# A gated attention and spatial-gating block on one core: reciprocal roots of the norms on GpSimd instead of VectorE and ScalarE

## The chip, the cores and the metric

The kernel runs on one core of one Trainium2 chip. The metric is the device time of one execution in microseconds; lower is better. The engines are named as the profile names them: PE (TensorE, matmuls; PEld is its weight load), DVE (VectorE), ACT (ScalarE), POOL (GpSimd) and SP (SyncE, which here only issues DMAs). Each engine takes its instructions in the order in which they stand in its own queue, and waits on semaphores for the others.

## The reference

One layer of a hybrid block on a sequence of 1024 rows of 1024 features, all in float32. Three norms take a reciprocal root, and they are what the change is about.

```python
def rmsnorm(x, g):
    y = xf * lax.rsqrt(jnp.mean(xf * xf, axis=-1, keepdims=True) + EPS)
    return (y * g)

def layernorm(x, g, b):
    xc = xf - mean(xf)
    return xc * lax.rsqrt(jnp.mean(xc * xc, axis=-1, keepdims=True) + EPS) * g + b

def reference(...):
    h = rmsnorm(x, norm_g)                             # norm 1
    q, k, v, za, u, vs, zs, gm = split(h @ w_in)
    a = window_sink_attention(rope(q), rope(k), v, sinks)
    a = (a * silu(za)) @ w_att_out
    sgo = gelu(u) * (mix(layernorm(gelu(vs))) + b)     # norm 2
    sgo = (sgo * silu(zs)) @ w_sg_out
    ga, gs = sigmoid(gm + b_merge)
    x = x + (ga * a + gs * sgo) @ w_o
    return rmsnorm(x, final_g)                         # norm 3
```

## The kernel before

Rows are handled in eight tiles of 128 (`NT` = 8, P = 128 partitions). A float32 matrix product is made of three matmuls of reduced-precision parts: each operand is split into a high part (a cast, on ACT, L155 or L554) and a low part (the difference, on DVE, L156 or L555), and PE multiplies high by high, high by low and low by high. The larger products go through `gemm_pair` (L350), which makes a two-by-two block product with seven instead of eight block products; its operands are sums, made beforehand. A scheduling layer places the instructions: the source fixes what depends on what, and the layer decides in which order the instructions of each engine stand, from its own estimates of what each costs. `after` (L158) adds an order between two instructions where the source asks for one.

The stages that touch the three norms:

- *Start.* Four dummy matmuls (`keep_busy`, L498) and the spreading of the gain row over partitions (L505). For each row tile t, `scale_of` (L528) squares the tile on ACT and sums the squares (L531, with a read of the accumulator), and `rstd_of` (L130) makes the reciprocal root; `normed_tile` (L537) scales the two halves of the tile on DVE (L545), PE transposes them (L551, two PSUM banks in turn), ACT and DVE make the high and low part (L554, L555), and ACT keeps an unsplit copy (L558, or L615 for tile 0). `vs_gemm` (L588) multiplies the first half of the `vs` columns with each tile: 24 matmuls (L596), whose result ACT copies out (L597). The weights for it are split in `split_vs` (L573): the first quarter in two halves, one on DVE and one on POOL (L583), the other three by L155 and L156.
- *Middle.* The second half of the `vs` columns is one long run of matmuls (L565). GELU follows on ACT (L637, L701), then the statistics per row on DVE (L633, L737), `normalize` (L739) with one reciprocal root for all eight tiles at once (128x8), and eight scalings (L742). The mixing matmuls (L764) read the result. Meanwhile POOL issues DMAs that add up weight blocks (L296), paced so that each waits for a given step of PE or ACT.
- *End.* The output product runs in four passes p of two row tiles each, seven block products a pass. After each block product `add_and_square` (L1582) adds the residual on DVE (L1584), squares the half on ACT and sums it (L1586); the first half's sum is scaled and offset (L1593), the second half's goes into `rstd_of` with the first as its base. `scale_and_store` (L1596) multiplies by root and gain (L1606 on DVE) and stores; in the last pass one half of each tile has its gain multiplied beforehand on POOL (L1589) and takes the root on ACT (L1603). The stores of the first three passes are issued by POOL, those of the last one by SP and ACT.

`rstd_of` is a chain over two engines: scale and offset on DVE (L133), square root on ACT (L135), reciprocal on DVE (L137), and a refining step on DVE (L140 to L145) that makes up for the table's error. Where ACT's loaded table does not hold the function that comes next, a table load stands ahead of it; the first, for the root, is brought forward by a dummy (L108).

Of the kernel before, what the change touches and what calls it, by code (L numbers as in the profile page):

```python
# [24 lines left out]
F32 = mybir.dt.float32  # L25
F32R = mybir.dt.float32r
AF = mybir.ActivationFunctionType
ALU = mybir.AluOpType
PSUM = bass.MemoryType.PSUM

P = 128
D = 1024
# [3 lines left out]
NT = S // P  # L36
HD = 64
EPS = 1e-6
# [14 lines left out]
def hybrid_tile(  # L53
# [16 lines left out]
    nc = tc.nc  # L70

    dram = ctx.enter_context(tc.tile_pool(name="dram", bufs=1, space=bass.MemoryType.DRAM))
    const = ctx.enter_context(tc.tile_pool(name="const", bufs=1))
# [5 lines left out]
    def nm(s):  # L79
        count[0] += 1  # L80
        return f"{s}_{count[0]}"

    def bank(tag, dt=F32):
        return psum.tile([P, 512], dt, name=nm("ps_" + tag), tag="ps_" + tag, bufs=2)

    def mtile(shape, dt, tag, bufs, pool=None):
        return (pool or main).tile(shape, dt, name=nm(tag), tag=tag, bufs=bufs)
# [16 lines left out]
    make_identity(nc, ident[:])  # L104
    eps_sb = const.tile([P, 1], F32, name="eps_sb")
    nc.gpsimd.memset(eps_sb[:], EPS)
    warm = const.tile([P, 1], F32, name="warm")
    nc.scalar.activation(warm[:], eps_sb[:], AF.Sqrt)  # L108

    sink_sb = const.tile([P, 8], F32, name="sink_sb")  # L110
    nsink_sb = const.tile([P, 8], F32, name="nsink_sb")
# [15 lines left out]
    a_dr = scratch("a_dr")  # L127
    y_dr = scratch("y_dr")

    def rstd_of(ss, scale, base=EPS, n=1):  # L130

        ve = mtile([P, n], F32, f"st{n}", 16 if n == 1 else 5)
        nc.vector.tensor_scalar(ve[:], ss, scale, base, op0=ALU.mult, op1=ALU.add)  # L133
        rt = mtile([P, n], F32, f"st{n}", 16 if n == 1 else 5)
        nc.scalar.activation(rt[:], ve[:], AF.Sqrt)  # L135
        r0 = mtile([P, n], F32, f"st{n}", 16 if n == 1 else 5)
        nc.vector.reciprocal(r0[:], rt[:])  # L137
        e = mtile([P, n], F32, f"st{n}", 16 if n == 1 else 5)
        if n == 1:
            nc.vector.scalar_tensor_tensor(e[:], ve[:], r0[:], r0[:], op0=ALU.mult, op1=ALU.mult)  # L140
        else:
            nc.vector.tensor_mul(e[:], ve[:], r0[:])
            nc.vector.tensor_mul(e[:], e[:], r0[:])
        nc.vector.tensor_scalar(e[:], e[:], -0.5, 1.5, op0=ALU.mult, op1=ALU.add)
        nc.vector.tensor_mul(e[:], e[:], r0[:])  # L145
        return e

    def split(hi, lo, src, minus=False):
        if minus:
# [8 lines left out]
    def after(second, first):  # L158

        tc.add_manual_dep(  # L160
            second.ins,
            first.ins.name,
            mybir.DependencyInfo(mybir.DependencyClass.NoSync, mybir.DependencyReason.DATA),
            reason="order",
        )
# [5 lines left out]
    def slot(name, shape=(P, 4, HALF), dt=F32R):  # L171

        return mtile(list(shape), dt, "T_" + name, 1)
# [309 lines left out]
    mv = mtile([P, NT, 2], F32, "mv", 1, gelu)  # L483

    def load_x(t):
        xt = raw_tile()
        nc.sync.dma_start(xt[:], x[t * P : (t + 1) * P, :])
        return xt

    x_in = {0: load_x(0)}  # L490
    junk = mtile([P, D], F32, "wl", 3)
# [23 lines left out]
    f = {n: slot(at, dt=F32) for n, at in (("f11", "t3l"), ("f21", "t4l"))}  # L515
# [12 lines left out]
    def scale_of(t):  # L528
        xt = x_in[t] if t in x_in else load_x(t)
        ss = mtile([P, 1], F32, "st1", 16)  # L530
        square = nc.scalar.activation(junk[:], xt[:], AF.Square, accum_out=ss[:])  # L531
        if t == 1:

            after(square, casts[-1])
        return xt, rstd_of(ss[:], 1.0 / D)

    def normed_tile(t, scale=None):  # L537
        xt, r = scale or scale_of(t)
# [67 lines left out]
    x_in[1] = load_x(1)  # L606
    split_vs(1)
    second = scale_of(1)
    for c in (2, 3):
        load_vs(c)  # L610
# [126 lines left out]
        nc.vector.bn_aggr(mv[:, t, :], stats[:, t])  # L737

    def normalize():  # L739
        r = rstd_of(mv[:, :, 1], 1.0, n=NT)  # L740
        for t in range(NT):
            nc.vector.tensor_scalar(  # L742
                xh[:, t, :], xh[:, t, :], mv[:, t, 0:1], r[:, t : t + 1], op0=ALU.subtract, op1=ALU.mult
            )
# [574 lines left out]
    def gtag(among=4):  # L1319
        turn[0] += 1  # L1320
        return f"g{turn[0] % among}"
# [249 lines left out]
    for p in range(4):  # L1571
        n, t, acc, x11 = N_PAIRS + p, T_ORDER[p], accs[p], firsts[p]
# [3 lines left out]
        sq = {}  # L1576
# [5 lines left out]
        def add_and_square(i, half, src, sign):  # L1582
            z = xr[:, 2 * i + half, :]
            pace[0] = (nc.vector.tensor_sub if sign < 0 else nc.vector.tensor_add)(z, z, src)  # L1584
            ss = mtile([P, 1], F32, "st1", 16)
            nc.scalar.activation(bank("tp")[:], z, AF.Square, accum_out=ss[:])  # L1586
            if p == 3 and i == half:
                scaled[i, half] = mtile([P, HALF], F32, gtag(), 1, pool)
                nc.gpsimd.tensor_tensor(scaled[i, half][:], z, g_out[:, half, :], op=ALU.mult)  # L1589
            if i in sq:  # L1590
                sq[i] = rstd_of(ss[:], 1.0 / D, sq[i][:])
            else:
                nc.vector.tensor_scalar(ss[:], ss[:], 1.0 / D, EPS, op0=ALU.mult, op1=ALU.add)  # L1593
                sq[i] = ss

        def scale_and_store(i, p=p, t=t, xr=xr, sq=sq, scaled=scaled):  # L1596
# [34 lines left out]
        def by_t3():  # L1631
            product(acc, ready[n, 4], ob["t3"], False)
            make_sums(nc.vector.tensor_add(x22[:], x22[:], acc))
            add_and_square(1, 1, x22[:], -1.0)
# [111 lines left out]
```

## Time and profile before

| | us |
|---|---|
| three runs | 923.66, 924.23, 921.37 |
| their median | 923.66 |
| span of the profiled execution | 921.3 |
| PE busy in it | 904.7 |
| DVE busy | 691.5 |
| ACT busy | 521.8 |
| POOL busy | 126.8 |

The page states no time of the profiled execution beside its span; of the three runs the shortest, 921.37, is about as long as that span. Times in the views count from the start of the span. A row of the timeline gives start, duration, engine, line, operation, output and input, and in brackets how long the engine had been idle and what released it; rows of small operations that stand together can be merged (x2, x8). A row of the grouped view gives the busy time in total, the mean of one in nanoseconds, and the idle time ahead of the group with its releaser. The chain of waits is followed back from the last instruction.

### The profile page before, as it was taken

To read this page: it belongs to the slowest core of one execution; us is meant where nothing else is said; L and a number is where in the kernel's file an instruction comes from. 1 tells how busy PE (TensorE), PEld (TensorE's weight loads), DVE (VectorE), ACT (ScalarE), POOL (GpSimd) and SP (SyncE) were. 2 spreads that over 40 slices of the span, in tenths; PEclk is the share of its full clock that TensorE was granted. 3 is DMA by queue.
4 is the path that set the end of the run, shared out by engine and by line. 5 is a ranking of instruction groups with operands and counts; after the bars stand their busy time and mean duration, and the time that the engine had idled before them with its cause. 6 is when DMAs were issued, how large, how long until landed. Compare 5 with 4: busy or idle time off the path is not lost.

```text
span 921.3 us, 13177 instructions
## 1 busy us (share of the span) xinstructions
PE 904.7 (98%) x4332; PEld 752.7 (82%) x4332; DVE 691.5 (75%) x1241; ACT 521.8 (57%) x1046; POOL 126.8 (14%) x188
## 2 busy tenths in 40 slices
PE   8999999999999999999999999999998999999996
PEld 5888888888888788888888888888877887878885
DVE  6875776656687668887778888747798589579996
ACT  6862443334444366767766766755665385367443
POOL 0002122213011001211101111101100111110012
PEclk9999999999999999999999999999999999999998
DMA  6427678877788676776786799689869755998632
GB/s 240 138 91 215 207 197 184 161 158 234 230 290 267 229 200 182 169 202 184 197 240 222 248 220 253 174 313 349 294 219 341 240 201 151 272 307 303 206 115 114
DMA packets 128734, 201.71 MB, mean 219 GB/s; under 512 B 12345, under 2 KB 60729, under 8 KB 128666
## 3 DMA queue, kind: packets, MB, share of 16 engines
q1 hardware_dynamic: 109512, 148.17, 48.8%
q0 software_dynamic: 19008, 52.44, 23.8%
q8 instruction: 34, 0.56, 0.3%
q14 instruction: 34, 0.28, 0.1%
q10 hardware_dynamic: 146, 0.27, 0.1%
HBM read 144.07 MB, written 86.11 MB: 250 GB/s over the span
## 4 chain that ended last, share of the span: by engine, by line
PE 85%; DVE 8%; DMA 4%; issue 2%; ACT 1%; SPq 1%; DVEq 0%; ACTq 0%
PE ps_mm L341 34%; PE ps_o L341 25%; PE ps_mm L596 5%; PE ps_sc L1076 3%; PE ps_o L1161 2%; PE ps_tp L341 2%; PE ps_tp L1120 2%; PE ps_sc L341 2%; PE ps_tp L764 2%; DVE wl L156 1%; PE ps_tp L565 1%; PE ps_sc L565 1%; PE ps_o L565 1%; PE ps_mm L565 1%; DVE bq L185 1%
## 5 line engine op out<-in xcount | busy, mean ns | idle before, releaser
L155 ACT CAST wh<-s 128x1024 fp32r<-128x1024 f32 (+1 forms) x78 | 78.1, 1005 | 87.2 <-PE ps_mm L341 49.9
L156 DVE TENSOR_TENSOR wl<-wr,wh 128x1024 fp32r<-128x1024 f32 (+1 forms) x80 | 75.7, 948 | 49.1 <-ACT wh L155 48.3
L155 ACT CAST wh<-wr 128x1024 fp32r<-128x1024 f32 (+1 forms) x80 | 66.3, 830 | 71.6 <-PE ps_mm L341 34.3
L156 DVE TENSOR_TENSOR wl<-s,wh 128x1024 fp32r<-128x1024 f32 (+1 forms) x78 | 90.9, 1166 | 9.3 <-ACT wh L155 9.2
L341 PE MATMUL ps_o<-T_t1h,wh 128*128 128x512 f32 x148 | 58.9, 398 | 0.8 <-ACT wh L155 0.7
L341 PE MATMUL ps_o<-T_b22h,wh 128*128 128x512 f32 x148 | 58.2, 394 | 0.0
L341 PE MATMUL ps_o<-T_t1h,wl 128*128 128x512 f32 x148 | 57.9, 391 | 0.3 <-DVE wl L156 0.3
L341 PE MATMUL ps_o<-T_b22l,wh 128*128 128x512 f32 x148 | 57.9, 391 | 0.0
L341 PE MATMUL ps_o<-T_b22h,wl 128*128 128x512 f32 x148 | 57.8, 390 | 0.0
L341 PE MATMUL ps_o<-T_t1l,wh 128*128 128x512 f32 x148 | 57.6, 390 | 0.0
L341 PE MATMUL ps_mm<-T_b11h,wl 128*128 128x512 f32 x140 | 54.8, 392 | 2.9 <-DVE wl L156 2.9
L341 PE MATMUL ps_mm<-T_t4h,wh 128*128 128x512 f32 x140 | 55.3, 395 | 0.5 <-DVE x L376 0.5
L341 PE MATMUL ps_mm<-T_t3l,wh 128*128 128x512 f32 x140 | 54.6, 390 | 0.6 <-DVE T_t3l L156 0.6
L341 PE MATMUL ps_mm<-T_t2h,wl 128*128 128x512 f32 x140 | 55.0, 393 | 0.0
L341 PE MATMUL ps_mm<-T_t2l,wh 128*128 128x512 f32 x140 | 55.0, 393 | 0.0
L341 PE MATMUL ps_mm<-T_b11h,wh 128*128 128x512 f32 x140 | 54.9, 392 | 0.0
L341 PE MATMUL ps_mm<-T_t3h,wh 128*128 128x512 f32 x140 | 54.9, 392 | 0.0
L341 PE MATMUL ps_mm<-T_t2h,wh 128*128 128x512 f32 x140 | 54.7, 391 | 0.0
L341 PE MATMUL ps_mm<-T_t4h,wl 128*128 128x512 f32 x140 | 54.7, 391 | 0.0
L341 PE MATMUL ps_mm<-T_t3h,wl 128*128 128x512 f32 x140 | 54.7, 390 | 0.0
L341 PE MATMUL ps_mm<-T_b11l,wh 128*128 128x512 f32 x140 | 54.6, 390 | 0.0
L1089 ACT ACTIVATE pr<-ps_sc,sm 128x192 f32<-128x192 f32 (+2 forms) x128 | 50.9, 410 | 6.5 <-DVE sm L1085 5.5
(356 smaller groups left out, 2399.6 us busy)
## 6 DMA issues: line engine op xcount, KB each, us to landing
wr<-in_w_dram SPq DMA_DIRECT2D x86, 256.0 KB
sums<-in_w_dram POOLq DMA_DIRECT2D x20, 512.0 KB, 5.6
s<-sums SPq DMA_DIRECT2D x20, 512.0 KB
q_hl<-qhl SPq DMA_DIRECT2D x16, 512.0 KB
q<-q_hl SPq DMA_DIRECT2D x64, 128.0 KB
wr<-in_w_dram SPq DMA_DIRECT2D x14, 512.0 KB
y_dr<-x POOLq DMA_DIRECT2D x28, 256.0 KB, 6.6
g<-in_w_dram POOLq DMA_DIRECT2D x12, 512.0 KB, 7.2
```

Of the source, the lines that this page charges most:

```text
L155: nc.scalar.copy(hi, src)
L156: return nc.vector.tensor_sub(lo, src, hi.bitcast(F32))
L185: op(dst[:, i : i + 2, :], a[:, i : i + 2, :], c[:, i : i + 2, :])
L341: nc.tensor.matmul(acc, lt, rt, start=fresh and k == 0 and n == 0, stop=k == 3 and n == 2, skip_group_check=True,)
L565: mm = nc.tensor.matmul(acc, lt, rt, start=k == 0 and n == 0, stop=k == KC - 1 and n == 2)
L596: nc.tensor.matmul(acc[:], lt, rt, start=k == 0 and n == 0, stop=k == KC - 1 and n == 2)
L764: nc.tensor.matmul(pm[:, t * P : (t + 1) * P], xh[:, half * 4 + t, g * P : (g + 1) * P], bias[-1][1][:, g % 4, :], start=True, stop=True,)
L1076: nc.tensor.matmul(sc[:, i, k0:], q_of[:, c, i * P : (i + 1) * P], kt[:, f, k0:], start=f == 0, stop=f == 1,)
L1089: nc.scalar.activation(held_in[c, i], sc[:, i, lo:hi], AF.Exp, bias=nmax[:, c, i : i + 1], scale=-1.0, accum_out=sums[:, c, i : i + 1],)
L1120: nc.tensor.transpose(dst, pr[:, i, block * P : block * P + width], ident[:])
L1161: nc.tensor.matmul(po[:, cs], lt, rt, start=n == 0, stop=n == len(terms) - 1)
```

## The change

The reciprocal root is made on POOL by an addition of the offset and a power with exponent -0.5, the exponent read from a small tile filled once. The division by the number of features goes into the scale that ACT applies before it squares. The refining step, the square root on ACT and the reciprocal are gone. The dummy that loads a table at the start now asks for GELU's. The first half's sum in the last norm takes its offset on POOL too. In the built program the scheduling layer has placed the instructions of the start anew on every engine; from the first `gemm_pair` on the order is the same but for the operations named here, one sum (L245) that now stands behind the scalings L742, and the squares L1586 that stand ahead of the copies L1614 at the end of a pass.

```diff
     nc.gpsimd.memset(eps_sb[:], EPS)
+    power = const.tile([P, NT], F32, name="power")
+    nc.gpsimd.memset(power[:], -0.5)
     warm = const.tile([P, 1], F32, name="warm")
-    nc.scalar.activation(warm[:], eps_sb[:], AF.Sqrt)
+    nc.scalar.activation(warm[:], eps_sb[:], AF.Gelu)
...
-    def rstd_of(ss, scale, base=EPS, n=1):
-
-        ve = mtile([P, n], F32, f"st{n}", 16 if n == 1 else 5)
-        nc.vector.tensor_scalar(ve[:], ss, scale, base, op0=ALU.mult, op1=ALU.add)
-        rt = mtile([P, n], F32, f"st{n}", 16 if n == 1 else 5)
-        nc.scalar.activation(rt[:], ve[:], AF.Sqrt)
-        r0 = mtile([P, n], F32, f"st{n}", 16 if n == 1 else 5)
-        nc.vector.reciprocal(r0[:], rt[:])
-        e = mtile([P, n], F32, f"st{n}", 16 if n == 1 else 5)
-        if n == 1:
-            nc.vector.scalar_tensor_tensor(e[:], ve[:], r0[:], r0[:], op0=ALU.mult, op1=ALU.mult)
-        else:
-            nc.vector.tensor_mul(e[:], ve[:], r0[:])
-            nc.vector.tensor_mul(e[:], e[:], r0[:])
-        nc.vector.tensor_scalar(e[:], e[:], -0.5, 1.5, op0=ALU.mult, op1=ALU.add)
-        nc.vector.tensor_mul(e[:], e[:], r0[:])
-        return e
+    def rstd_of(ms, base=EPS, n=1):
+
+        r = mtile([P, n], F32, f"st{n}", 16 if n == 1 else 5)
+        nc.gpsimd.tensor_scalar_add(r[:], ms, base)
+        nc.gpsimd.tensor_tensor(r[:], r[:], power[:, 0:n], op=ALU.pow)
+        return r
+
+    ROOT = D**-0.5
...
-        square = nc.scalar.activation(junk[:], xt[:], AF.Square, accum_out=ss[:])
+        square = nc.scalar.activation(junk[:], xt[:], AF.Square, scale=ROOT, accum_out=ss[:])
...
-        return xt, rstd_of(ss[:], 1.0 / D)
+        return xt, rstd_of(ss[:])
...
-        r = rstd_of(mv[:, :, 1], 1.0, n=NT)
+        r = rstd_of(mv[:, :, 1], n=NT)
...
-            nc.scalar.activation(bank("tp")[:], z, AF.Square, accum_out=ss[:])
+            nc.scalar.activation(bank("tp")[:], z, AF.Square, scale=ROOT, accum_out=ss[:])
...
-                sq[i] = rstd_of(ss[:], 1.0 / D, sq[i][:])
+                sq[i] = rstd_of(ss[:], sq[i][:])
             else:
-                nc.vector.tensor_scalar(ss[:], ss[:], 1.0 / D, EPS, op0=ALU.mult, op1=ALU.add)
+                nc.gpsimd.tensor_scalar_add(ss[:], ss[:], EPS)
                 sq[i] = ss
```

## The prediction

> **What bounds the kernel now.** The page first: how long, who is busy, which chain ended last. Then the list of what TensorE (PE) waited for, up to 64 us and from 64 to 906 us (microseconds in total, times, longest).
>
> ```profile
> span 921.3 us, 13177 instructions
> ...
> PE 904.7 (98%) x4332; PEld 752.7 (82%) x4332; DVE 691.5 (75%) x1241; ACT 521.8 (57%) x1046; POOL 126.8 (14%) x188
> ...
> PEclk9999999999999999999999999999999999999998
> ...
> PE 85%; DVE 8%; DMA 4%; issue 2%; ACT 1%; SPq 1%; DVEq 0%; ACTq 0%
> ...
> PE ps_sc L498 <- DVE T_b22l L494: 1.9, 1, 1.9
> PE ps_tp L551 <- issue: 0.5, 1, 0.5
> ...
> PE ps_mm L341 <- DVE wl L156: 2.9, 2, 1.7
> ```
>
> PE is the bound. Up to 64 us it waited at its first dummy matmul and, for 0.5 us, at the transposes of the first row tile; its longest waits afterwards are for a weight split far from the change. So the change reaches the end at two places only: before PE has its first real operand, and after its last matmul. In between, small operations on VectorE (DVE) and ScalarE (ACT) are worth something only where PE would have to wait.
>
> The start, from the timeline (start, duration, engine, line, output and input):
>
> ```profile
> 3.92 3.78 PE L505 MATMUL ps_o<-wh,wl 1*128 1x512 f32 x4
> ...
> 5.39 0.18 ACT L531 ACTIVATION_READ_ACCUMULATOR wl<-wr 128x1 f32 x1
> ...
> 6.68 0.16 DVE L145 TENSOR_TENSOR st<-st,st 128x1 f32<-128x1 f32 x1
> ...
> 7.19 1.40 POOL L583 TENSOR_TENSOR T_t1l<-T_t3h,T_t1h 128x512 fp32r<-128x512 f32 x1 [5.88 <-ACT T_t1h L582]
> 7.37 1.40 DVE L545 SCALAR_TENSOR_TENSOR wr<-wr,st,ps_o 128x512 f32<-128x512 f32 x2
> 7.99 1.05 ACT L155 CAST T_t1h<-T_t3h 128x1024 fp32r<-128x1024 f32 x1 [0.89 <-DMA T_t3h<-in_w_dram]
> ...
> 8.21 1.94 PE L551 MATMUL ps_tp<-ident,wr 128*128 128x128 f32 x8 [0.52 <-issue]
> 9.07 1.23 DVE L156 TENSOR_TENSOR T_t1l<-T_t3h,T_t1h 128x1024 fp32r<-128x1024 f32 x1 [0.30 <-ACT T_t1h L155]
> 9.34 0.59 ACT L554 CAST T_b11h<-ps_tp 128x512 fp32r<-128x512 f32 x1 [0.30 <-PE ps_tp L551]
> ...
> 9.97 1.22 PE L596 MATMUL ps_mm<-T_t1h,T_b11h 128*128 128x512 f32 x2
> ...
> 10.22 0.68 DVE L555 TENSOR_TENSOR T_b11l<-ps_tp,T_b11h 128x512 fp32r<-128x512 f32 x1
> ...
> 10.67 1.06 ACT L531 ACTIVATE wl<-wr 128x1024 f32<-128x1024 f32 x1
> ...
> 10.99 0.89 PE L596 MATMUL ps_mm<-T_t1l,T_b11h 128*128 128x512 f32 x2
> ...
> 11.72 1.04 ACT L155 CAST T_t2h<-T_t4h 128x1024 fp32r<-128x1024 f32 x1
> 11.72 0.62 PE L596 MATMUL ps_mm<-T_t1h,T_b11l 128*128 128x512 f32 x2
> ...
> 13.56 0.61 PE L596 MATMUL ps_mm<-T_t2h,T_b21h 128*128 128x512 f32 x2
> ...
> 16.78 1.20 PE L551 MATMUL ps_tp<-ident,wr 128*128 128x128 f32 x8
> ...
> 18.11 0.73 PE L596 MATMUL ps_mm<-T_t1h,T_b11h 128*128 128x512 f32 x2
> ```
>
> One chain is to be seen: tile 0's sum of squares (5.57), the root's small steps (6.84), the scaling L545 at 7.37, transposes at 8.21, cast L554 at 9.34, first matmul at 9.97. DVE scales *before* it turns to the split L156 at 9.07, which needs a transfer and the cast of 7.99. After that the chain of waits is nothing but PE (72 matmuls in 16.34 us, 0.227 us each; eight transposes 0.87 us):
>
> ```profile
> 45.09 0.87 PE ps_tp L551 x8
> 45.96 16.34 PE ps_mm L596 x72
> ```
>
> The end, timeline again:
>
> ```profile
> 911.92 1.28 POOL L1589 TENSOR_TENSOR g<-bq,bq 128x512 f32<-128x512 f32 x1 [0.38 <-DVE bq L1584]
> ...
> 913.76 0.16 DVE L145 TENSOR_TENSOR st<-st,st 128x1 f32<-128x1 f32 x1
> 913.83 0.68 DVE L1584 TENSOR_TENSOR bq<-bq,ps_mm 128x512 f32<-128x512 f32 x1
> 914.01 0.72 ACT L1603 ACTIVATE g<-g,st 128x512 f32<-128x512 f32 x1 [0.93 <-DVE st L145]
> ...
> 914.64 0.58 ACT L1586 ACTIVATE ps_tp<-bq 128x512 f32<-128x512 f32 x1
> ...
> 915.16 0.19 ACT L1586 ACTIVATION_READ_ACCUMULATOR ps_tp<-bq 128x1 f32 x1
> ...
> 916.70 0.75 DVE L1606 SCALAR_TENSOR_TENSOR bq<-bq,st,bq 128x512 f32<-128x512 f32 x1
> ```
>
> From the last sum of squares (915.35) to the last scaling (916.70) lie 1.35 us, all of them the root.
>
> **The change part by part.** *The price of the new root.* It is two GpSimd (POOL) instructions on one column, an addition and, after a wait for it, a power. No row shows either. The nearest:
>
> ```profile
> L106 POOL MEMSET eps_sb<- 128x1 f32 x1 | 0.1, 100 | 0.0
> L1589 POOL TENSOR_TENSOR g<-bq,bq 128x512 f32<-128x512 f32 x2 | 2.9, 1450 | 4.0 <-DVE bq L1584 4.0
> ...
> L137 DVE RECIPROCAL st<-st 128x1 f32<-128x1 f32 x16 | 2.5, 157 | 1.4 <-ACT st L135 1.4
> ```
>
> Below, 0.10 us each, the POOL fill of one column; above, 1.45 us, a POOL product over 512 columns. I take 0.2 us for the addition (twice the fill: it also reads) and 0.5 us for the power (nearer to the one-column row in width, but it is no plain product), and 0.05 us for each of three handovers: 0.85 us from sum to scaling, between 0.35 (both at 0.10) and 1.8 (power at 1.45). Before, it took 1.35 us at the end.
>
> The GPSIMD Engine Reference of the Trainium skill (section "Performance versus the Vector engine") speaks against the move: ordinary elementwise work runs about half as fast there as on VectorE. No run here shows it for one column; by it, an estimate of twice the 0.157 us row for each of the two, the root would take 0.78 us and the sum below would be lower by 0.14 us.
>
> *The start.* The order in which the changed kernel's instructions stand differs here, and that decides. On DVE the splits L583 and L156 now stand ahead of tile 0's L545. L156 still waits for the cast of 7.99 to 9.04, so it still runs from 9.07, and the next DVE operation begins at 10.22, as L555 does now. L545 thus moves from 7.37 to about 10.24, by 2.87 us. The power hides under that: on POOL it stands behind the split L583, which starts by 7.19 and ends by 8.59, so even at 1.45 us the root is there at 10.1. Behind L545 the distances stay: transposes at 11.08, first matmul at 12.84. Bound: ACT now casts T_t2h ahead of L554; that cast may begin as late as 11.72 as in the trace, and would then hold L554 to 12.8 instead of 12.21: 0 to +0.55 us, and I take 0, since the row's cast waited for ACT, not for its data.
>
> What PE does with the delay. Its first twelve matmuls take 3.59 us (9.97 to 13.56): 12.84 to 16.43, two more to 16.88. Then stand tile 1's transposes (earlier than now: inside the first product). ACT's order is L554, T_t2h, the other L554 (to 14.2), square L531 to 15.30; the root at +0.85 gives L545 at 16.15, its first half (0.72) to 16.87, the transposes at 16.97: +0.1 us. The same walk over tiles 2 to 4 gives 0.1, 0.6 and 0.4 us, the last two since tile 3's and 4's transposes wait for a PSUM bank whose last reader, the copy L558, waits for DVE's L555, which stands behind the next tile's L545 and so behind its root. That loop turns in about 4.5 us (square 1.25, root 0.85, L545 and L555 0.7 each, two copies 0.5 each as ACT's casts follow each other), and a tile of PE work is 24 × 0.227 + 0.87 = 6.3 us, so from tile 5 on PE sets the pace again. Added waits: 1.2 us.
>
> What falls away: today PE loses 18.11 − 16.78 − 0.87 = 0.46 us between tile 1's transposes and their cast, and some 0.2 us at T_t2l; both have their operands early in the new order. Start: 2.87 + 1.2 − 0.66 = **+3.4 us**; from +2.1 (root 0.35, no added wait but 0.1, less 0.66, and 0.2 more hidden) to +5.4 (root 1.8: about one us more over tiles 1 to 4; the cast 0.55; 0.4 for what I walked coarsely).
>
> *The middle.* The norm of the mixing branch is one addition and one power on eight columns, standing on POOL on either side of one of its DMA issues. The rows are a table load, the first use of the norm, and PE's first use of what it made:
>
> ```profile
> L135 ACT ACT_TABLE_LOAD x2 | 2.6, 1283 | 0.0
> ...
> 113.70 2.26 DVE L742 TENSOR_SCALAR xh<-xh,mv,st 128x1024 f32<-128x1024 f32 x3
> ...
> 123.08 1.78 PE ps_tp L764 x16
> ```
>
> DVE is free for L742 some 1.5 us before 113.70, since the root's five small steps (0.16 each) and the sum L245 (0.7) no longer stand ahead of it; so much may POOL's issue and power take before anything is later than now, and PE needs xh only at 123.08. Worth 0: PE does not wait there; without that cover it would cost the root's 0.85 us once. L245's result is cast only after PE has reached the mixing, so its move costs 0. POOL's later DMA issues wait for PE and ACT themselves, so the 0.7 us of roots moves none of them by more than that. SP's queue swaps two pairs of input loads, each with a tile of slack. Four table loads of 1.28 us on ACT (at L637, twice at L135, at L792) go; all stand under a busy PE: 0.
>
> *The end.* PE ends where it did, so L1584 still runs 913.83 to 914.51. POOL's L1589 ends at 913.20, and only then come tile 0's addition and power: root at 914.00 (913.92 now), L1603 at 914.05, last square at 914.66 (914.64 now), its sum at 915.37. Root 0.85, last scaling at 916.22 instead of 916.70: **−0.5 us**; with 0.35 −1.0, with 1.8 also L1603 is late (914.98, square 915.6): +1.4. In the three earlier passes squares and scalings have a whole pass of PE work (seven products of 2.72 us) as cover: 0.
>
> *Sum.* 3.4 − 0.5 = +2.9 us on the span of 921.3: 924.2. The page gives no time of its own for that execution; one run of three took 921.37, their median is 923.66, 2.4 us more. On the median: 926.6, from +1.1 (924.8) to +6.8 (930.5).
>
> **The rivals.** *Clock.* The first four matmuls take 0.5 and 0.37 us each (9.97 to 10.99 to 11.72), later ones 0.23; the granted clock reads full (the PEclk line), yet PE is slow for 1.7 us after starting. The change widens the idle stretch before the transposes from 0.52 to 3.4 us (7.70 to 11.08). If today's release owes something to the work before 7.70, the slow stretch grows by up to that idle, 3 us, of which half is lost: +1.5 us, 928.1. For: the release came only 3.5 us after the transposes began. Against: the work before 7.70 had not released it, so it may count for nothing. TensorE: Matmul & The Clock Gate of the Trainium skill (Part 1) says just this: half rate after an idle window of about 3.4 us, full after a busy one. The trace agrees with the two rates (0.51 and 0.23), not with a release by the first 5.8 us of work.
>
> *A slow power.* If POOL's power takes 3 us, twice its costliest row, the root takes 3.35. Tile 0's comes at 11.7 (8.59 and 3.1), 1.45 late; tile 1's sum then comes at 16.75, its L545 at 20.1, 2.6 after PE wants it; 0.5 more for tile 2: start 2.87 + 1.45 + 2.6 + 0.5 − 0.66 = 6.8. At the end root, L1603, square and root in a row, 913.2 + 3.3 + 0.6 + 0.75 + 3.35 = 921.2, +4.5: 935.0. It outweighs everything from a power of 1.5 us on. For: a power is no plain arithmetic. Against: POOL's plain rows cost 2.5 ns a column.
>
> *Not slower.* The delay at the start is taken up by the 2.9 us that PE waits for L156 later on, if those waits end by a transfer's own clock and not by PE's progress: 926.6 − 2.9 = 923.7, and with the cheap root (start +2.1, all of it taken up) 923.66 − 1.0 = 922.7. It decides once all 2.9 us are taken up. For: DMA has 4% of the chain. Against: these loads are issued as buffers come free, which follows PE.
>
> *The change does not do what it says*: a table still loaded in the middle. It would show as a row and cost 0, under PE.
>
> **How the numbers follow.** Forecast 0.55 (926.6, its own range 924.8 to 928.5), clock 0.12, slow power 0.13, not slower 0.2. About 0.3%, 2.8 us, is what a measurement of this kernel can tell from no change. The bound is then 926.4, just under the forecast: slower 0.55 × 0.5 + 0.1 + 0.13 = 0.51; faster (under 920.9) only out of the last rival with a cheap root and the runs' own spread of 2.9 us, 0.11; the rest 0.38. The range, 922.3 to 931.0, leaves out the slow power and the luckiest runs.
>
> **What would show it.** L545 of tile 0 after L156, near 10.2; first matmul near 12.8; the 72-matmul stretch ending near 65.7 instead of 62.30; POOL's two root rows, 0.7 us together; last scaling 0.5 us sooner behind PE's end. Wrong if the first matmul still starts near 10, if the vs products end before 63.5, or if the power's row is over 1 us.

## The result and the profile after

| | before | after |
|---|---|---|
| median, us | 923.37 (921.37 to 927.14, 12 runs) | 927.08 (925.24 to 928.68, 12 runs) |
| ratio | | 1.0031, 95% interval 1.0018 to 1.0045 |
| span of the profiled execution | 921.3 | 924.4 |
| DVE, ACT, POOL busy | 691.5, 521.8, 126.8 | 679.6, 514.3, 149.2 |

The changed kernel is slower by 0.3%, 3.7 us between the medians and 3.1 us between the two profiled executions. The forecast was 926.6 on the median and 2.9 us on the span. Wherever a run's span is on record, its time is 1.7 to 1.9 us longer than the span. So the profiled execution of 921.3 belongs to a run of about 923.1 us, near the median, and not to the one of 921.37; most of the 2.4 us that the prediction puts between span and median is this difference, which both kernels have. The page of the changed kernel:

```profile
span 924.4 us, 13117 instructions
...
PE 903.6 (98%) x4332; PEld 751.9 (81%) x4332; DVE 679.6 (74%) x1147; ACT 514.3 (56%) x1025; POOL 149.2 (16%) x231
```

DVE and ACT lost 12 and 7.5 us of work, and it bought nothing, since neither was the bound. (In the changed kernel most line numbers are 7 lower: L545 is now L538, L156 is L149.) The chain of waits of the changed kernel, start and duration, has the 72 matmuls by which the start is measured:

```profile
49.61 16.35 PE ps_mm L589 x72
```

They end at 65.96, against 62.30 before: 3.66 us, more than the whole loss. Where it is made is seen in two views. First the windows: limits, length, PE's busy time with its number of instructions, granted clock, DMA share and rate; the kernel before, then the changed one.

```profile
8.00:62.30 54.30, 53.94 (x257) 1.00 0.44 153
```

```profile
8.00:65.96 57.96, 54.53 (x257) 1.00 0.40 137
```

The same 257 matmuls took 0.59 us longer, and PE stood idle for 3.43 instead of 0.36 us. (The granted clock of 1.00 says nothing about the first microseconds: the trace's record of it begins at 11.55 us before and at 14.90 after, and time without a record counts as full.) The list of what PE waited for up to 65.96 us in the changed kernel (total, times, longest) names the idle time:

```profile
PE ps_tp L544 <- DVE wr L538: 2.5, 1, 2.5
PE ps_sc L491 <- DVE T_b22l L487: 1.9, 1, 1.9
PE ps_tp L544 <- ACT T_t4l L551: 0.9, 2, 0.6
PE ps_tp L544 <- ACT T_t3h L551: 0.3, 1, 0.3
```

The 1.9 us were there before; new are 2.5 us ahead of the first transposes and 1.2 us at later ones (the second halves of tiles 3, 4 and 5), whose PSUM bank ACT's copy had not yet read. The timeline of the changed kernel's start:

```profile
7.00 1.26 POOL L576 TENSOR_TENSOR T_t1l<-T_t3h,T_t1h 128x512 fp32r<-128x512 f32 x1 [0.99 <-ACT T_t1h L575]
7.04 1.31 DVE L677 TENSOR_SCALAR ones<-ident 128x128 fp32r<-128x128 f32 x1
7.21 1.04 ACT L148 CAST T_t1h<-T_t3h 128x1024 fp32r<-128x1024 f32 x1 [0.30 <-DMA T_t3h<-in_w_dram]
8.22 0.56 POOL L136 TENSOR_TENSOR st<-st,power 128x1 f32<-128x1 f32 x1
8.29 1.23 DVE L149 TENSOR_TENSOR T_t1l<-T_t3h,T_t1h 128x1024 fp32r<-128x1024 f32 x1
9.43 1.40 DVE L538 SCALAR_TENSOR_TENSOR wr<-wr,st,ps_o 128x512 f32<-128x512 f32 x2
...
10.23 1.97 PE L544 MATMUL ps_tp<-ident,wr 128*128 128x128 f32 x8 [2.55 <-DVE wr L538]
...
12.02 1.22 PE L589 MATMUL ps_mm<-T_t1h,T_b11h 128*128 128x512 f32 x2
...
13.04 1.05 PE L589 MATMUL ps_mm<-T_t1l,T_b11h 128*128 128x512 f32 x2
...
13.89 1.05 PE L589 MATMUL ps_mm<-T_t1h,T_b11l 128*128 128x512 f32 x2
...
14.74 0.70 PE L589 MATMUL ps_mm<-T_t1h,T_b11h 128*128 128x512 f32 x2
...
15.28 0.63 PE L589 MATMUL ps_mm<-T_t1l,T_b11h 128*128 128x512 f32 x2
```

The split L149 stands ahead of the scaling L538, as forecast; the power ends at 8.78, beside L149, and is not what the scaling waits for. The transposes begin at 10.23 instead of 8.21. And PE's slow stretch, in which a pair takes over 1 us, lasts from 12.02 to about 15 us, where before it ended at 11.72. One row has moved. The filling of the tile `ones` stood behind the first matmuls in the kernel before:

```profile
11.42 0.22 DVE L684 TENSOR_SCALAR ones<-ident 128x128 fp32r<-128x128 f32 x1
```

Now it stands ahead of L149 and took 1.31 us. It costs nothing here, because L149 needs the cast of 7.21 to 8.25, but it comes back below.

The timeline of the changed kernel's end:

```profile
915.11 1.29 POOL L1582 TENSOR_TENSOR g<-bq,bq 128x512 f32<-128x512 f32 x1
...
916.38 0.28 POOL L135 TENSOR_SCALAR st<-st,st 128x1 f32<-128x1 f32 x1
916.74 0.57 POOL L136 TENSOR_TENSOR st<-st,power 128x1 f32<-128x1 f32 x1
917.00 0.69 DVE L1577 TENSOR_TENSOR bq<-bq,ps_mm 128x512 f32<-128x512 f32 x1 [2.03 <-PE ps_mm L334]
917.34 0.72 ACT L1596 ACTIVATE g<-g,st 128x512 f32<-128x512 f32 x1 [1.56 <-POOL st L136]
...
917.97 0.58 ACT L1579 ACTIVATE ps_tp<-bq 128x512 f32<-128x512 f32 x1
...
918.49 0.19 ACT L1579 ACTIVATION_READ_ACCUMULATOR ps_tp<-bq 128x1 f32 x1
...
918.78 0.30 POOL L135 TENSOR_SCALAR st<-st,st 128x1 f32<-128x1 f32 x1 [1.47 <-ACT ps_tp L1579]
919.16 0.57 POOL L136 TENSOR_TENSOR st<-st,power 128x1 f32<-128x1 f32 x1
...
919.76 0.75 DVE L1599 SCALAR_TENSOR_TENSOR bq<-bq,st,bq 128x512 f32<-128x512 f32 x1 [1.41 <-POOL st L136]
```

From the last sum (918.68) to the last scaling lie 1.08 us: addition 0.30, power 0.57, and 0.21 for three handovers. Before they were 1.35. From the last residual addition to the last scaling it is 2.76 us (917.00 to 919.76), before 2.87 (913.83 to 916.70): 0.11 us won. The three pieces add up: +3.66 at the start, −0.49 between (913.83 − 62.30 = 851.53 against 917.00 − 65.96 = 851.04), −0.11 at the end, 3.06 of the 3.1 us.

The −0.49 is not won by the change. Windows again, over the piece between, the kernel before, then the changed one, and a short one out of the kernel before:

```profile
62.30:913.83 851.53, 845.00 (x4068) 1.00 0.75 224
```

```profile
65.96:917.00 851.04, 843.26 (x4068) 1.00 0.76 224
```

```profile
325.58:328.99 3.41, 3.41 (x12) 0.50 0.90 208
```

In the profiled execution of the kernel before the granted clock fell to half once, for 3.41 us, and in that of the changed kernel never: PE was busy 1.74 us less there, and it waited 1.25 us more (7.78 against 6.53). Seven of the thirteen profiled executions have such falls, as is shown below; that the two spans differ by about as much as the medians is in part chance.

### The profile page after: what moved, and what is told of

Its sections match the earlier page's. It is cut to its first block, busy times and chain, and to the rows that moved or that the text cites. A ratio compares the mean times of both kernels' runs of the same rounds, so it can differ in the third digit from the quotient of the medians.

```text
span 924.4 us, 13117 instructions
## 1 busy us (share of the span) xinstructions
PE 903.6 (98%) x4332; PEld 751.9 (81%) x4332; DVE 679.6 (74%) x1147; ACT 514.3 (56%) x1025; POOL 149.2 (16%) x231
## 4 chain that ended last, share of the span: by engine, by line
PE 81%; DVE 8%; DMA 5%; issue 2%; ACT 2%; SPq 1%; POOL 0%; POOLq 0%; DVEq 0%; ACTq 0%
PE ps_mm L334 34%; PE ps_o L334 25%; PE ps_mm L589 3%; PE ps_sc L1069 3%; PE ps_o L1154 2%; PE ps_sc L334 2%; PE ps_tp L334 2%; PE ps_tp L1113 2%; DMA wr<-in_w_dram 2%; DVE wl L149 1%; PE ps_tp L757 1%; PE ps_tp L558 1%; PE ps_sc L558 1%; PE ps_o L558 1%; PE ps_mm L558 1%
## 5 line engine op out<-in xcount | busy, mean ns | idle before, releaser
L149 DVE TENSOR_TENSOR wl<-wr,wh 128x1024 fp32r<-128x1024 f32 (+1 forms) x80 | 75.8, 948 | 52.3 <-ACT wh L148 51.5
L149 DVE TENSOR_TENSOR wl<-s,wh 128x1024 fp32r<-128x1024 f32 (+1 forms) x78 | 90.9, 1167 | 10.9 <-ACT wh L148 10.7
```

The costliest lines, as they stand in the source:

```text
L149: return nc.vector.tensor_sub(lo, src, hi.bitcast(F32))
```

## The experiments

Theory: the loss is made at the start, by the late first scaling, a longer slow stretch of PE and the root's loop through the PSUM banks; the new root itself is cheap. Rivals: that the loss lies in the middle or at the end, that the power's own latency makes it, that it is the clock. Each of the following was timed in five rounds beside the kernel before. The columns: start of tile 0's first scaling, first matmul of the first product, end of the 72-matmul stretch, span of the profiled execution, medians of the kernel and of the one before beside it, and their ratio with its interval.

| kernel | scaling | matmul | stretch ends | span | median, before | ratio |
|---|---|---|---|---|---|---|
| old root at the start | 7.34 | 9.95 | 62.31 | 923.2 | 924.08, 924.37 | 0.9991 (0.9979 to 1.0003) |
| new root only at the start | 9.37 | 11.96 | 65.47 | 923.4 | 928.54, 924.37 | 1.0042 (1.0029 to 1.0056) |
| scaling first | 8.29 | 10.87 | 63.94 | 921.1 | 925.20, 924.37 | 1.0006 (0.9993 to 1.0018) |
| old root, scaling late | 10.12 | 12.72 | 66.33 | 924.8 | 928.33, 924.37 | 1.0039 (1.0024 to 1.0053) |
| ones later | 7.24 | 9.95 | 62.06 | 920.2 | 921.35, 923.67 | 0.9968 (0.9956 to 0.9980) |
| power twice | 10.89 | 13.47 | 69.37 | 929.8 | 930.53, 923.67 | 1.0071 (1.0059 to 1.0083) |
| dummy matmuls | 9.30 | 11.88 | 65.64 | 925.5 | 926.77, 923.67 | 1.0031 (1.0020 to 1.0042) |
| first split behind the scaling too | 6.89 | 10.06 | 62.87 | 920.2 | 922.05, 923.67 | 0.9987 (0.9975 to 0.9999) |
| third weight piece before tile 1 | 7.03 | 10.35 | 64.17 | 922.2 | 923.59, 923.68 | 0.9999 (0.9987 to 1.0011) |
| ones later alone | 10.57 | 13.16 | 67.58 | 928.9 | 927.88, 923.68 | 1.0052 (1.0037 to 1.0067) |
| ones later, again | 7.01 | 9.60 | 62.41 | 921.2 | 922.59, 923.68 | 0.9989 (0.9978 to 1.0000) |

### Which place: the start, or the rest

```diff
-        return xt, rstd_of(ss[:])
+        return xt, old_rstd_of(ss[:], 1.0 / D)
```

`old_rstd_of` is the root of the kernel before; the square of the start has no scale, and the first dummy loads the root's table.

> The eight row tiles of the start take the old root (ScalarE's root and VectorE's five steps, the root's table loaded first); the mixing and the end keep the new one. Theory (the loss is all made at the start, by the later first scaling, the longer slow clock and the root's loop): the 72-matmul stretch ends near 62.3 us as before instead of 65.96, and the time is 923.2 to 923.7, 0.996 of the changed kernel's, within 0.5 us of the kernel before. Rival (the loss is made, or made again, in the middle or at the end, by GpSimd's slower root there): the stretch ends near 62.3, but the span stays above 923.

The start is again that of the kernel before (in the first 60 us PE, DVE, ACT and SP have the same rows in the same order), and the median is 0.3 us under it. The one profiled span of 923.2 is above the 923 that the rival names; 2.0 us of that lie between the stretch and PE's end (the last residual addition at 915.82, 853.5 us behind the stretch instead of 851.5). That is no sign of the rival: in this execution the granted clock fell to half twice, from 325.74 and from 701.21 us for 3.41 us each, and PE was busy there for 846.37 us instead of 845.00. The eleven timed runs agree: the loss is not made in the middle or at the end. The mirror, with the old root in the mixing and at the end only (there without the square's scale):

```diff
-        r = rstd_of(mv[:, :, 1], n=NT)
+        r = old_rstd_of(mv[:, :, 1], 1.0, n=NT)
...
-                sq[i] = rstd_of(ss[:], sq[i][:])
+                sq[i] = old_rstd_of(ss[:], 1.0 / D, sq[i][:])
```

> The mirror of the run above: only the start takes the new root, the mixing and the end take the old one (two table loads more on ScalarE). Theory: the 72-matmul stretch ends near 66.0 and the time is that of the changed kernel plus the 0.1 us that the end won, ratio to before 1.003 to 1.004. Rival (middle or end are what costs): ratio below 1.001.

It has the whole loss, 1.0042, just above the expected 1.004, and its start has the changed kernel's order. Both runs say the same: start.

### Which mechanism: the order, or the new root

In the changed kernel, an edge each puts DVE's split L149 behind the two scalings, and POOL's half split behind the first power. The lists hold instructions in the order of the source: `scalings` two for each tile, `splits` DVE's half, POOL's half, and then the second, third and fourth weight piece, `roots` the powers.

```diff
+    after(splits[1], roots[0])
+    after(splits[2], scalings[1])
     second = scale_of(1)
```

> The changed kernel, with two order edges: VectorE's split of the second weight piece stands behind the first tile's two scalings, and GpSimd's split behind the first power. Theory (the order is what moved the first scaling, and the power itself is cheap): first scaling near 7.2 instead of 9.43, first matmul near 9.9 instead of 12.0, first twelve matmuls in 3.6 instead of 4.2 us, the 72-matmul stretch 2 us or more earlier than 65.96; time 924.0 to 925.3. Rival (the loop over root, scaling, copy and PSUM bank sets the pace of the first tiles whatever the order): first matmul early, but the 72-matmul stretch still ends at 65.3 to 66, time 926 to 927.

The ratio falls to 1.0006 with the new root everywhere: order makes most of the loss. The first scaling came earlier, but at 8.29, not 7.2. The timeline of that kernel shows what held it, since its root was there at 6.65:

```profile
6.08 0.57 POOL L138 TENSOR_TENSOR st<-st,power 128x1 f32<-128x1 f32 x1
...
7.02 1.26 POOL L580 TENSOR_TENSOR T_t1l<-T_t3h,T_t1h 128x512 fp32r<-128x512 f32 x1 [0.37 <-ACT T_t1h L579]
7.07 1.30 DVE L683 TENSOR_SCALAR ones<-ident 128x128 fp32r<-128x128 f32 x1
...
8.29 1.39 DVE L542 SCALAR_TENSOR_TENSOR wr<-wr,st,ps_o 128x512 f32<-128x512 f32 x2
```

The `ones` again, 1.30 us, ending 0.09 us after POOL's split. The counterpart is the kernel before with its old root, where only the two scalings are put behind the split:

```diff
+    after(scalings[0], splits[2])
+    after(scalings[1], splits[2])
     second = scale_of(1)
```

> The kernel before, with one thing changed: the first tile's two scalings stand behind VectorE's split of the second weight piece, as they do in the changed kernel; the root is the old one. Theory: order alone makes most of the loss: first scaling near 9.4 to 10.3, the 72-matmul stretch ending 1.5 to 3 us after 62.30, ratio to before 1.0015 to 1.0035. Rival (the new root's latency makes the loss, not the order): later waits take the delay up, the stretch ends within 0.7 us of 62.30, ratio below 1.001.

```profile
8.98 1.22 DVE L156 TENSOR_TENSOR T_t1l<-T_t3h,T_t1h 128x1024 fp32r<-128x1024 f32 x1 [0.27 <-ACT T_t1h L155]
10.12 1.40 DVE L547 SCALAR_TENSOR_TENSOR wr<-wr,st,ps_o 128x512 f32<-128x512 f32 x2
```

Without any new root, 1.0039: at least the size of the whole change, and more than the upper 1.0035 expected. The scaling at 10.12 is 0.69 later than in the changed kernel, because the split's cast began at 7.90 instead of 7.21, with the weight transfer. So an order with the late scaling is enough for the loss, and mending it is enough to lose most of it. What is shown is the order as a whole, not the place of two instructions: from the one edge the layer has placed more of the start anew (`ones` stands beside POOL's split here too, and tile 1's transposes begin at 19.07 instead of 16.78 before and 16.68 in the changed kernel).

### The held operation

With the scaling first, one edge more:

```diff
-    nc.vector.tensor_scalar(ones[:], ident[:], 0.0, 1.0, op0=ALU.mult, op1=ALU.add)
+    after(nc.vector.tensor_scalar(ones[:], ident[:], 0.0, 1.0, op0=ALU.mult, op1=ALU.add), scalings[1])
```

> The kernel with the scaling first, and one more order edge: VectorE's small making of the tile of ones stands behind the first tile's scalings. Theory (in three runs that operation took 1.30 us beside GpSimd's split and ended 0.08 to 0.09 us after it, against 0.22 us in the kernel before: VectorE is held until GpSimd's split is over, and the first scaling behind it): ones takes 0.2 us, the first scaling starts at 7.1 to 7.2 instead of 8.29, the first matmul near 9.8 instead of 10.87, the 72-matmul stretch ends near 62.9, time 0.9988 to 1.0000 of the kernel before. Rival (the operation is long for a reason of its own, or the tiles behind set the pace): ones still takes over 1 us, or the stretch ends within 0.3 us of 63.94 and the ratio stays at 1.0006.

```profile
7.20 1.27 POOL L580 TENSOR_TENSOR T_t1l<-T_t3h,T_t1h 128x512 fp32r<-128x512 f32 x1 [0.64 <-ACT T_t1h L579]
7.24 1.40 DVE L542 SCALAR_TENSOR_TENSOR wr<-wr,st,ps_o 128x512 f32<-128x512 f32 x2
...
8.37 1.05 ACT L150 CAST T_t1h<-T_t3h 128x1024 fp32r<-128x1024 f32 x1 [1.25 <-DMA T_t3h<-in_w_dram]
...
11.55 0.63 PE L593 MATMUL ps_mm<-T_t1h,T_b11l 128*128 128x512 f32 x2
...
11.79 0.21 DVE L683 TENSOR_SCALAR ones<-ident 128x128 fp32r<-128x128 f32 x1
```

Away from POOL's split the filling takes 0.21 us, and the scaling, which reads one operand from PSUM, runs beside that split at its usual 0.7 us a half. The stretch ends at 62.06, before the old kernel's 62.30, and the ratio of 0.9968 is the best of all, below the expected 0.9988. It is also more than the trace accounts for (1.1 us of span against 2.3 between the medians), so the same kernel was taken once more:

> The kernel with the ones later once more, with the two above, since its ratio of 0.9968 is more than its trace shows (0.24 us at the start, 0.1 us at the end, 0.75 us between, 1.1 us of span in all, against 3.0 us). Theory (the trace's 1.1 us): 0.9980 to 0.9995. Rival (all of the ratio): 0.9960 to 0.9975.

```profile
7.06 1.05 ACT L150 CAST T_t1h<-T_t3h 128x1024 fp32r<-128x1024 f32 x1 [0.18 <-DMA T_t3h<-in_w_dram]
...
13.88 0.63 PE L593 MATMUL ps_mm<-T_t1h,T_b11l 128*128 128x512 f32 x2
```

0.9989, with an interval that touches 1. The two intervals meet only between 0.9978 and 0.9980, so the measured gain over the kernel before is some 0.1 to 0.3%, of which the trace explains about 0.1%. Much of the rest goes with the granted clock, which is on record for each timed run: on the mean 0.9972 in the first taking against 0.9956 of the kernel before beside it, 0.9964 against 0.9960 in the second. Runs of one kernel differ by 0.6 to 1.2 us for each 0.001 of it; by that estimate 1.0 to 1.9 of the 2.7 us between the means of the first taking, and 0.2 to 0.5 of the 0.9 us of the second, are the clock's. For the losses it is no rival: with the new root only at the start it was 0.9952 against 0.9953, with the old root and the scaling late 0.9950 against 0.9953. This version beats the changed kernel clearly (by 0.4 to 0.6%, from 1.0031) and the kernel before by little. No kernel here has the new root with the old order of the start row for row: the layer places PE's later transposes otherwise in each.

That the `ones` are not the loss itself was tried in the changed kernel, with that edge and nothing else:

> The changed kernel with the tile of ones made behind the first scalings, and nothing else moved: the split of the second weight piece stays ahead of the scalings. Theory: the 1.3 us of the ones lie under the wait for that piece's cast (ended at 8.25 in the changed kernel), so first scaling and the 72-matmul stretch move by no more than the piece's landing does (first scaling within 0.1 us of the split's end), time 0.999 to 1.001 of the changed kernel, 1.002 to 1.004 of the one before. Rival (the ones are what costs 3.7 us): ratio to before below 1.001.

The first scaling (10.57) still follows the split (from 9.43 for 1.23 us in that run), and the ratio is 1.0052, above what was expected; the transfer came late in the profiled execution (cast at 8.35), and the granted clock of the timed runs, 0.9950 against 0.9960, is worth some 0.6 to 1.2 us by the estimate above. Two disturbances stood one behind the other, and moving the second alone shows nothing.

### What the root's own latency is worth

```diff
+        if n == 1:
+            nc.gpsimd.tensor_tensor(spare[:], r[:], power[:, 0:n], op=ALU.pow)
         nc.gpsimd.tensor_tensor(r[:], r[:], power[:, 0:n], op=ALU.pow)
```

> The changed kernel with the power of every one-column root taken twice on GpSimd (the first into a spare tile that nothing reads): each root is 0.57 us longer, nothing else is moved. Theory: tile 0's second power still lies under VectorE's split (first scaling 9.43 to 9.5), tiles 1 to 4 lose some of their 0.6 us each in the loop over root, scaling and PSUM bank (72-matmul stretch ends 0.5 to 2 us after 65.96), and the end loses 0.6 us at each of the last two roots; 1.0015 to 1.0035 of the changed kernel, 928.5 to 930.3. Rival (the root lies beside other work): within 0.5 us of the changed kernel, first and last scalings where they were.

Measured 1.0071 to before, 1.0040 on the changed kernel's 1.0031, 3.7 us, above the 1.0035 expected. At the end the mechanism is as the theory has it:

```profile
921.17 0.69 DVE L1581 TENSOR_TENSOR bq<-bq,ps_mm 128x512 f32<-128x512 f32 x1 [2.03 <-PE ps_mm L338]
...
925.17 0.75 DVE L1603 SCALAR_TENSOR_TENSOR bq<-bq,st,bq 128x512 f32<-128x512 f32 x1 [2.29 <-POOL st L140]
```

4.00 us instead of 2.76, twice 0.62. At the start the stretch ended 3.41 us later, of which 1.46 are the late first scaling (10.89 against 9.43; its cast waited for the transfer till 8.67, not for the power). The other 1.95 hold a longer wait for the banks (2.7 instead of 1.2 us) and 0.2 at another scaling. Those waits are at the second halves of tiles 2 to 5. (The layer has also moved one scaling on DVE and, by one matmul each, two groups of transposes on PE.) So the power's latency is on the path in the loop over the banks, in this order: with the ones later, the same new root and another order of PE's transposes, PE waited for a bank not at all in one execution and for 0.3 us in the other, and with the old root (the kernel before, and with the scaling late) not at all.

### Idle time and the slow stretch of PE

Four more dummy matmuls behind the broadcast of the gains (`bc` is its last matmul):

```diff
     keep_busy(2)
+    for _ in range(4):
+        after(nc.tensor.matmul(idle[:], ones_r[:, 0:P], ones_r[:], start=True, stop=True), bc)
```

> The changed kernel with four dummy matmuls behind the broadcast of the gains, which fill 2.1 of the 2.5 us in which TensorE waits for the first scaling. Theory of the clock (the slow rate lasts longer because TensorE stood idle): the slow matmuls fall from six or seven to at most four, the first twelve take 3.6 us or less instead of 4.2, the stretch ends 0.5 to 1.0 us before 65.96, time 0.9990 to 0.9996 of the changed kernel. Rival (the slow rate has nothing to do with that idle time): first twelve matmuls 4.1 to 4.3 us, the stretch within 0.2 us of 65.96.

```profile
10.09 1.97 PE L546 MATMUL ps_tp<-ident,wr 128*128 128x128 f32 x8 [0.40 <-DVE wr L540]
...
11.88 1.01 PE L591 MATMUL ps_mm<-T_t1h,T_b11h 128*128 128x512 f32 x2
12.73 0.63 PE L591 MATMUL ps_mm<-T_t1l,T_b11h 128*128 128x512 f32 x2
```

The slow stretch was short, the first twelve matmuls took 3.14 us (11.88 to 15.02) instead of 4.19. Yet the 72-matmul stretch ended only 0.32 earlier, and the time is that of the changed kernel, 1.0031: what PE won it waited for later, 0.7 us at the second tile's transposes alone. Whether the dummies made the stretch short is open: the kernel with the ones later has it end at 11.55 in one execution and at 13.88 in the other, with PE idle for less than 0.4 us ahead of the transposes in both.

### Two attempts to win more

DVE's first half split behind the scalings as well:

```diff
+    after(splits[0], scalings[1])
```

> The kernel with the ones later, and the first half split on VectorE (0.69 us) also behind the first tile's scalings: these wait for the power alone. Theory: first scaling at 6.7, transposes near 7.75 as TensorE's broadcast ends, first matmul near 9.4, the 72-matmul stretch 0.3 to 0.6 us earlier than with the ones alone moved, time 0.9982 to 0.9996 of the kernel before. Rival (the split, now late, holds the third matmul, or later tiles set the pace): no earlier than the run with the ones later.

The scaling came at 6.89 and the transposes at 7.69, right behind the broadcast; but ACT was then casting weights that had landed late (8.48 to 9.53), and cast the transposed tile only behind that. First matmul 10.06, no better than 9.95, and the stretch ended at 62.87, later than in both executions with the ones later: the rival, though the ratio of 0.9987 lies in the theory's range. The last:

```diff
+    after(scalings[2], splits[3])
+    after(scalings[3], splits[3])
+    after(splits[4], scalings[3])
     normed_tile(2)
```

> The kernel with the ones later, and VectorE's first split of the third weight piece ahead of the second tile's scalings, the next split behind them. With the ones later TensorE still waited 0.7 us for that split (14.0 to 14.71). Theory (that wait is lost time): it falls under 0.2 us, the 72-matmul stretch ends 0.4 to 0.7 us before 62.06, ratio 0.0003 to 0.0008 below the run with the ones later that is timed beside it. Rival (the second tile's scalings, now later, cost as much): the stretch within 0.3 us of 62.06 or later.

The wait for the third weight piece was gone, as the theory said, but the stretch ended at 64.17 and the ratio is 0.9999 (0.9989 beside it): the rival. Only part of the 2.11 us on 62.06 is the edit, since PE's slow pairs lasted until 16.29 in this execution.

## Why the prediction came out right

*The price of the root.* Forecast 0.85 us between 0.35 and 1.8; measured 1.08. Addition 0.2 against 0.30 at the end (0.22 at the start), power 0.5 against 0.57, handovers 0.15 against 0.21. By an estimate from the rule of the GPSIMD Engine Reference of the Trainium skill (section "Performance versus the Vector engine") the root would have taken 0.78; the addition fits it (0.30 against twice 0.157), the power does not, at 3.6 times the reciprocal's 0.157. A power near 3 us, as in the rival, is there only for the eight columns of the mixing, under PE; the group's row of the changed kernel (total, mean in ns, idle):

```profile
L136 POOL TENSOR_TENSOR st<-st,power 128x8 f32<-128x8 f32 x1 | 2.7, 2674 | 0.0
```

*The first scaling.* Right in its mechanism, the order, which the pair "scaling first" and "old root, scaling late" shows. Its size was off: forecast from 7.37 to 10.24 and transposes at 11.08, measured 9.43 and 10.23, so +2.02 for PE instead of 2.87. The step that failed is "it still runs from 9.07": L156 runs when its weights have landed, and the casts that wait for them began anywhere from 7.02 (dummy matmuls) to 8.76 us (third weight piece before tile 1), at 7.06 and 8.37 with the same kernel. The `ones`, which the prediction's order leaves out, ended with the cast and cost nothing. In the six profiled kernels where the scaling stands behind that split it came at 9.30 to 10.89; in front of it, with the ones out of the way, at 6.89 to 7.37. That is what the order really does: it ties the first tile to a transfer that has no fixed time.

*The added waits* of 1.2 us are 1.2 us of idle time, in the bank loop as described, but at tiles 3, 4 and 5 (0.60, 0.28 and 0.33) instead of 1 to 4; the chain of waits takes the last of them back to a row tile's transfer (27.29 to 31.31), for which ACT waited 0.28 us. They cost more than they show as idle time: a matmul's row lasts 0.39 us while the next starts 0.227 behind it, so PE has lost time before its rows show a gap. By starts (when the next matmul was due and when it came) they cost 0.76, 0.44 and 0.49, together 1.7 us.

*What falls away.* Forecast −0.66, reckoned by starts, and by starts it is −0.65: in the kernel before 1.33 us pass from tile 1's first transpose to the next matmul (16.78 to 18.11), where eight transposes take 0.87, and two pairs at T_t2l were 0.06 and 0.17 late; the changed kernel has neither. As idle time only 0.15 of it shows.

*The clock* was counted at 0 and given as a rival of +1.5; the longer slow stretch cost 0.60 in this execution (the first twelve matmuls took 4.19 us, 12.02 to 16.21, instead of 3.59). Its cause, idle time, was not confirmed.

So the start's 3.66 is 2.02 + 0.60 + 1.7 − 0.65, within rounding, where the forecast had 2.87 + 0 + 1.2 − 0.66. The path was right; that the sum came out is luck, since the scaling's 0.85 too much cancels most of the 1.1 us that clock and waits had too little.

*The middle* was counted at 0 and is 0 within what can be seen. From the end of the stretch to the last residual addition it takes 849.8 us with the scaling first and 854.0 with the ones later alone, both with the same new root there; the windows of the two:

```profile
63.94:913.75 849.81, 843.27 (x4069) 1.00 0.76 224
```

```profile
67.58:921.54 853.96, 846.48 (x4069) 1.00 0.76 223
```

The second execution has two falls of the granted clock (from 331.33 and from 706.80 us), the first none. So it is in all thirteen profiled executions: PE is busy there for 843.1 to 843.3 us in the six without a fall, 844.5 to 845.0 in the five with one, 846.4 to 846.5 in the two with two, whatever the root. What is left, PE's waits, is 6.3 to 7.3 us in the three kernels with the old root there (before, new root only at the start, old root with the scaling late) and 6.1 to 9.2 in the others. The lost table loads win nothing that shows: with the old root in the mixing and at the end the ratio is 1.0042, without it 1.0031, and the intervals overlap.

*The end.* Forecast −0.5, measured −0.11. The sign was right; the root took 1.08 instead of 0.85, and the other tile's scaling L1596 came 0.94 behind POOL's product (916.40 to 917.34) instead of 0.85, so that the last square began 0.97 after the residual addition, not 0.83 as forecast (0.81 before).

*The rival "not slower"*, that later waits take up the delay, did not come: PE's waits behind 66 us that belong to weights are the same 2.9 us.

## What to carry over

Where a scheduling layer places the instructions, a change of one small operation can be worth less than the new order that comes with it; pin the order of the old kernel and measure again before judging the operation. At the start of a kernel, put what PE waits for ahead of work that waits for a transfer, on every in-order engine. Making other engines less busy was worth nothing here, with PE at 98%. And before two executions are compared, see how often the granted clock fell in each.

## What the runs showed of the hardware

*DVE held by POOL.* The filling of `ones` (DVE, one operand, both sides in SBUF) takes 0.21 to 0.22 us alone and 1.30 to 1.32 us when POOL's 128x512 subtraction began just before; it ends 0.08 to 0.09 us after that, in all six kernels where the two met. The scaling, with an operand in PSUM, is not held (0.70 us a half). It goes the other way too. With the scaling first, POOL's one-column addition took 0.77 instead of 0.22 us beside DVE's subtraction of two SBUF operands, and ended 0.08 after it:

```profile
15.05 2.35 DVE L151 TENSOR_TENSOR T_t2l<-T_t4h,T_t2h 128x1024 fp32r<-128x1024 f32 x2
...
16.71 0.77 POOL L137 TENSOR_SCALAR st<-st 128x1 f32<-128x1 f32 x1 [3.02 <-ACT wl L528]
```

SBUF — State Buffer of the Trainium skill (section "SBUF: two separate sides") states an exclusive lock on a pair of ports that DVE and POOL share, held for a whole instruction; these rows agree. One row does not fit its form: in the changed kernel L149 (two SBUF operands) began 0.07 us after POOL's power and took its usual 1.23 us.

*The slow stretch.* In it a matmul starts every 0.43 us (two from 13.04 to 13.89 in the changed kernel), later every 0.227. The trace's record of the granted clock begins with the full rate, at 11.55 us before and at 14.90 after, 3.3 and 4.7 us behind the first transposes; for one and the same kernel, the ones later, it is 3.2 (8.04 to 11.22) and 5.9 (7.80 to 13.68). Idle time ahead of it does not sort these. Further on the granted clock falls to half for 3.413 us at a time, once or twice in seven of the thirteen profiled executions, between 325 and 334 us and between 699 and 707 us. Each fall begins a whole number of times 3.413 us behind the first full rate (in the kernel before 314.03 us, 92 times), so a window of that length runs through the execution. TensorE: Matmul & The Clock Gate of the Trainium skill (Part 1) has a window of about 3.4 us that runs freely, whatever the kernel does, and full rate after a busy one; these records agree with such a window. By an estimate from that rule the start of the work would be followed by 3.4 to 6.8 us at half rate, which all four fit within 0.3 us. Two others do not by this count: 2.4 us with the dummy matmuls, where the dummies from 7.61 on would make it 4.9, and 8.2 with the third weight piece earlier (7.82 to 16.06), where PE paused for 0.56 us on the way. What counts as a pause was not tried.

A longer slow stretch need not cost what it seems to: of the two executions with the ones later the one with 5.9 us ended its 72-matmul stretch only 0.35 us after the other (62.41 and 62.06), which had waited 0.7 us for a weight split. A fall costs some 1.6 us of PE's time, by the three groups above. Why it comes in one execution and not in the next is open: both places lie shortly behind waits of PE of 1.4 to 1.8 us, which every execution has.
